# Prompt attention of a hybrid decoder layer: from one instruction stream per superblock to one stream over all superblocks

## The chip, the cores and the metric

One NeuronCore of a Trainium2 chip runs the whole kernel. The metric is the device time of one execution in microseconds (us): the median of several runs, lower is better. Where a trace is read, it is the trace of one profiled execution, whose own time is given beside it.

The engines are named as the profile names them: PE is TensorE (matrix products and transposes), PEld its weight loads, DVE is VectorE, ACT is ScalarE, POOL is GpSimd, and SP is SyncE, which only issues transfers here. SPq, POOLq and so on are the transfer queues that these engines issue to.

## The reference, cut to what matters

The reference is one inference step of one decoder layer over a prompt of 2048 tokens, with 16 learned meta tokens ahead of it, and over 8 x 8 sample tokens with a paged cache. Model width is 1024; there are 8 attention heads of 64 columns and a recurrent branch of 512 columns.

```python
def layer(x, attend, ...):
    hn = rmsnorm(x, g_mix_pre)
    q, k, v, xl, gate = jnp.split(hn @ w_in, [512, 1024, 1536, 2048], axis=-1)
    attn = attend(q, k, v)
    lru, h_last, conv_last = rglru_branch(xl, ...)
    mixed = jnp.concatenate([attn, lru * jax.nn.gelu(gate)], axis=-1) @ w_out
    x = x + rmsnorm(mixed, g_mix_post)
    u = jax.nn.relu(rmsnorm(x, g_mlp_pre) @ w_up)
    x = x + rmsnorm((u * u) @ w_down, g_mlp_post)

def sb_attend(q, q_pos, k, v, k_pos, bias):       # stick-breaking attention
    z = einsum('bqhd,bkhd->bhqk', q, k) * HEAD_DIM**-0.5 + bias
    mask = k_pos < q_pos
    log_keep = where(mask, log_sigmoid(-z), 0)
    suffix = cumsum(log_keep, axis=3, reverse=True) - log_keep
    w = where(mask, exp(log_sigmoid(z) + suffix), 0)
    return einsum('bhqk,bkhd->bqhd', w, v)
```

Attention is causal, and a weight is the product of a sigmoid with all later keep factors of its row. So keys are worked through from the last to the first, with a carry from one group of keys to the next. There is no softmax and no sum to divide by.

## The kernel before

The 2048 prompt rows are cut into four superblocks of `SB` = 512 rows (s = 0 to 3). Every float32 product is made as three products of a shorter type, high x high, high x low and low x high, so a weight tile (`wraw`) is loaded by SyncE and split into `whi` (ScalarE, L158) and `wlo` (VectorE, L159) first.

**Main stream.** It runs in this order: the input projections of superblocks 0 to 3 (`inproj`: recurrent branch and gates, keys, values, then queries); then, for each superblock, the output projection (`out_proj`), the transposes of its normed rows (`xpose`, L261), and the MLP in four slices (`up`, `down`). Its products are in `gemm` (L171 to L189; matmuls at L181, L182, L183: one tile of 512 columns takes 24 of them) and in `gemm_nat` (L191 to L224; L213, L214, L215). The keys and values of a superblock go to DRAM tiles `kd` and `vd`, its queries to `qd[s]`, and attention's output to `md[s]`, from which `load()` brings it back (`x<-md`, L955; cast to `ahi` on ScalarE at L951 and rest to `alo` at L952). The values leave their projection through `v_evac`: ScalarE copies a tile to a staging buffer `sf` (L561, stored to `out_v_prompt` by SyncE, L568) and casts it to `vst` (L564, stored to `vd`, L556).

**Side stream.** Attention is woven into the main stream. `Work` keeps a list `side` of generators, each with a key that it marks done at its end and a key that has to be ready before it starts. `work.tick(c)`, called by the products after every few matmuls, adds `c` times `work.rate` to a debt, and steps the present generator until the debt is paid; each step says how much of the debt it pays. `work.burst` steps for a given amount, and `work.need(key)` steps until `key` is done. Before the output projection of superblock s, `group(s)` calls `work.need(("a", s))`. The call for superblock 0 comes right after the first of the four query products of superblock 3. The list before is `sample_attn`, then `attn(0)` to `attn(3)`; `attn(s)` may start when `("kv", s)` is ready, which the end of superblock s's queries marks.

**One attention step.** For a head, `head()` loads its queries `q` (two buffers, L667) and its last 128 keys and values `kvt` (three buffers, L671, L672); `kv_load()` loads a group of 512 keys and values `kv` (three buffers, L684, L685, L691, L692). All of these are issued by GpSimd. Then, on each tile of 128 queries:

- logits: two matmuls into a bank `T` (L702; three banks, shared with the transposes);
- `chain`: two sigmoids on ScalarE (`keep` L640, `beta` L641), a scan on VectorE (L645, L648), the carry, and a product (L652);
- four steps later or more, `emit_T`: up to four transposes (L712) into another bank `T`, copied to `wth` by ScalarE (L723, or L719 for the group of 16 meta rows) and to `wtl` by VectorE (L724, or L720);
- four steps later or more, `emit_V`: two matmuls with the values (L734, L736) into the one bank `O`; after a head's last values ScalarE copies half of `O` (`pb`, L744), VectorE adds the other half, and SyncE stores the head to `md[s]` (L746).

A generator ends when its logits are used up and its queues of pending transposes (`tq`) and values (`vq`) are empty. So the last transposes and values of a superblock are issued before the first logits of the next.

The order on TensorE is that of the program text, with the side steps where `Work` puts them. The orders on ScalarE, VectorE, GpSimd and SyncE are made by a scheduler, which may issue a load ahead of its place in the text when its buffer is free.

Of the kernel before, what the change touches and what calls it, by code (L numbers as in the profile page):

```python
# [8 lines left out]
F32 = mybir.dt.float32  # L9
F32R = mybir.dt.float32r  # L10
# [6 lines left out]
P = 128  # L17
# [19 lines left out]
class Work:  # L37
# [7 lines left out]
    def step(self):  # L45
        while True:
# [5 lines left out]
            try:  # L52
                busy, pe = next(self.gen)
# [31 lines left out]
def _program(tc, I, O, NSB, NSC):  # L85
# [570 lines left out]
    def attn(s, K):  # L656
        live = {"w": 0, "kv": 0, "kvt": 0}
        tq, vq, heads = [], [], {}
        step = [0]

        def keys(h, a, n):
            return kd[h].rearrange("e p n -> (e p) n")[:, a:a + n]

        def head(h):
            if h < NH and h not in heads:
                q = T(att, [P, 2, SB], F32R, "q", 2)
                nc.gpsimd.dma_start(q.rearrange("p e n -> p (e n)"),  # L667
                                    qd[s][h].rearrange("p e n -> p (e n)").unsqueeze(0).to_broadcast([2, HD, 2 * SB]))
                kt = T(att, [P, 256], F32R, "kvt", 3)
                k0 = SB * s + 3 * P  # L670
                nc.gpsimd.dma_start(kt[:, 0:P], keys(h, NMETA + k0, P))  # L671
                nc.gpsimd.dma_start(kt[:, P:2 * P], vd[h, :, k0:k0 + P])  # L672
                live["kvt"] += 1
                heads[h] = {"q": q, "kt": kt, "carry": [None] * 4, "out": None}
            return heads.get(h)

        kvs = {}

        def kv_load(n):
            if n < len(groups) and n not in kvs:  # L680
                h, g = groups[n]
                t = T(att, [P, 1024], F32R, "kv", 3)
                if g == 0:
                    nc.gpsimd.dma_start(t[:, 0:400], keys(h, 0, 400))  # L684
                    nc.gpsimd.dma_start(t[:, 400:784], vd[h, :, 0:384])  # L685
                    nc.gpsimd.memset(t[:, 784:784 + P].bitcast(F32), 0.0)
                    for r in (0, 32):
                        nc.gpsimd.dma_start(t[r:r + NMETA, 784:784 + P], vmd[:, h])
                else:
                    k0 = SB * g - P  # L690
                    nc.gpsimd.dma_start(t[:, 0:512], keys(h, NMETA + k0, 512))  # L691
                    nc.gpsimd.dma_start(t[:, 512:1024], vd[h, :, k0:k0 + 512])  # L692
                kvs[n] = t
                live["kv"] += 1
# [599 lines left out]
```

## Time and profile before

| | us |
|---|---|
| runs | 2788.22, 2781.06, 2786.87 |
| median | 2786.87 |
| the profiled execution's own time | 2790.22 |
| its span | 2788.3 |
| TensorE busy | 2688.2 |
| VectorE busy | 1814.3 |
| ScalarE busy | 1451.6 |
| GpSimd busy | 515.5 |

The span is the time from the first to the last instruction of the profiled execution; its own time is 1.9 us longer. The mean granted clock of TensorE was 0.985 of full speed. The shares of busy time are means over stages with different limits: projections without attention, projections with attention, output projection, MLP with attention (until about 2147 us) and MLP alone. In the lines quoted below, `O<-wth,kv` is an instruction that writes `O` and reads `wth` and `kv`, `128*128 128x512` are the shapes of the operands, and `[2.98 <-DVE wth L720]` says that the engine had been idle for 2.98 us and that the VectorE instruction of line 720 ended this.

### The profile page before, as it was taken

The page shows a single profiled execution, that of the slowest core. Times are in us where ns is not written, and L with a number is a line of the kernel's source. Part 1 is how long each engine was busy: PE and PEld are TensorE (multiplying, and loading weights), DVE is VectorE, ACT ScalarE, POOL GpSimd, SP SyncE. Part 2 cuts the span into 40 slices and gives each one's busy share as a digit, 9 for nine tenths or more (in the row PEclk, how much of TensorE's full clock was granted, in tenths as well). Part 3 has the DMA queues.
Part 4 walks back from the last instruction along what each step waited for, and adds up shares of the span by engine and source line. Part 5 has one row for each costly group of instructions (what it writes and reads, how often), then busy time and mean ns, then how long its engine had stood idle before and what let it go on. Part 6 is the DMA issues. An engine that isn't in the chain of part 4 may idle for free.

```text
span 2788.3 us, 36998 instructions
## 1 busy us (share of the span) xinstructions
PE 2688.2 (96%) x13804; PEld 2219.4 (80%) x13804; DVE 1814.3 (65%) x2790; ACT 1451.6 (52%) x2426; POOL 515.5 (18%) x711
## 2 busy tenths in 40 slices
PE   8999988998899999999999999999999999999998
PEld 6886766777688888887788888878888887998996
DVE  5456364686777777788867777798686436433434
ACT  6556364575665655565555555665555234332332
POOL 5336361341211101112110001120000002000002
PEclk9999998999999999999999999999999999999999
DMA  4465855467534433345443333454333334322223
GB/s 161 134 208 189 261 152 171 134 169 221 166 92 128 119 115 106 106 138 154 154 110 115 103 111 103 138 162 143 105 96 104 112 119 144 99 84 77 83 84 113
DMA packets 177316, 368.23 MB, mean 132 GB/s; under 512 B 49153, under 2 KB 79361, under 8 KB 177137
## 3 DMA queue, kind: packets, MB, share of 16 engines
q1 hardware_dynamic: 103792, 287.35, 32.2%
q0 software_dynamic: 73344, 78.52, 11.3%
q8 instruction: 109, 1.79, 0.3%
q14 instruction: 71, 0.57, 0.1%
HBM read 305.51 MB, written 60.04 MB: 131 GB/s over the span
## 4 chain that ended last, share of the span: by engine, by line
PE 80%; DVE 7%; DMA 5%; POOL 3%; issue 3%; ACT 2%; SPq 0%; POOLq 0%; DVEq 0%; ACTq 0%
PE D L181 11%; PE D L183 11%; PE D L182 11%; PE D L213 10%; PE D L214 10%; PE D L215 10%; PE T L712 4%; PE T L702 4%; PE O L734 2%; PE O L736 2%; DVE wlo L159 1%; DMA md<-pb 1%; DVE pb L648 1%; POOL rstd L237 1%; DMA q<-qd 1%
## 5 line engine op out<-in xcount | busy, mean ns | idle before, releaser
L159 DVE TENSOR_TENSOR wlo<-wraw,whi 128x1024 fp32r<-128x1024 f32 x368 | 464.2, 1261 | 496.1 <-ACT whi L158 495.8
L181 PE MATMUL D<-ahi,whi 128*128 128x512 f32 (+3 forms) x1920 | 709.2, 369 | 0.0
L183 PE MATMUL D<-ahi,wlo 128*128 128x512 f32 (+3 forms) x1920 | 686.3, 357 | 2.0 <-DVE wlo L159 2.0
L182 PE MATMUL D<-alo,whi 128*128 128x512 f32 (+3 forms) x1920 | 685.0, 357 | 2.8 <-DVE alo L1017 1.5
L158 ACT CAST whi<-wraw 128x1024 fp32r<-128x1024 f32 x368 | 386.6, 1050 | 485.5 <-PE D L214 282.8
L213 PE MATMUL D<-whi,uh 128*128 128x512 f32 x1024 | 418.1, 408 | 0.0
L183 PEld LDWEIGHTS D<-ahi,wlo 128*128 128x128 f32 x1920 | 364.8, 190 | 53.2 <-DVE wlo L159 2.9
L181 PEld LDWEIGHTS D<-ahi,whi 128*128 128x128 f32 x1920 | 365.2, 190 | 51.9 <-issue 8.7
L214 PE MATMUL D<-whi,ul 128*128 128x512 f32 x1024 | 405.2, 396 | 0.0
L215 PE MATMUL D<-wlo,uh 128*128 128x512 f32 x1024 | 404.3, 395 | 0.0
L182 PEld LDWEIGHTS D<-alo,whi 128*128 128x128 f32 x1920 | 365.7, 190 | 45.5 <-DVE alo L1017 1.7
L640 ACT ACTIVATE keep<-T,nbias 128x512 f32<-128x512 f32 (+6 forms) x352 | 209.7, 596 | 241.7 <-PE T L702 234.6
L648 DVE TENSOR_TENSOR_SCAN pb<-keep,carry 128x513 f32<-128x513 f32 (+1 forms) x228 | 270.3, 1186 | 71.9 <-ACT keep L640 69.9
L724 DVE TENSOR_TENSOR wtl<-T,wth 128x512 fp32r<-128x512 f32 (+1 forms) x320 | 191.0, 603 | 73.7 <-ACT wth L723 72.6
L723 ACT CAST wth<-T 128x512 fp32r<-128x512 f32 (+1 forms) x320 | 166.1, 523 | 127.6 <-PE T L712 122.7
L215 PEld LDWEIGHTS D<-wlo,uh 128*128 128x128 f32 x1024 | 192.7, 188 | 46.7
L213 PEld LDWEIGHTS D<-whi,uh 128*128 128x128 f32 x1024 | 192.9, 188 | 39.9 <-DVE uf L1032 0.4
L214 PEld LDWEIGHTS D<-whi,ul 128*128 128x128 f32 x1024 | 193.3, 189 | 38.6
L652 DVE TENSOR_TENSOR beta<-beta,pb 128x512 f32<-128x512 f32 (+7 forms) x360 | 208.2, 578 | 0.0
L641 ACT ACTIVATE beta<-T,bias 128x512 f32<-128x512 f32 (+6 forms) x352 | 208.2, 591 | 0.0
L712 PE MATMUL T<-ident,beta 128*128 128x128 f32 (+1 forms) x1216 | 193.7, 277 | 14.1 <-ACT beta L641 7.6
L702 PE MATMUL T<-kv,q 128*128 128x512 f32 (+5 forms) x640 | 180.4, 364 | 10.3 <-ACT beta L641 4.4
(235 smaller groups left out, 3600.0 us busy)
## 6 DMA issues: line engine op xcount, KB each, us to landing
wraw<-in_w_up SPq DMA_DIRECT2D x128, 512.0 KB, 3.5
wraw<-in_w_down SPq DMA_DIRECT2D x128, 512.0 KB, 3.5
wraw<-in_w_in SPq DMA_DIRECT2D x64, 512.0 KB, 3.9
q<-qd POOLq DMA_DIRECT2D x32, 512.0 KB, 16.9
wraw<-in_w_out SPq DMA_DIRECT2D x32, 512.0 KB, 3.5
kv<-kd POOLq DMA_DIRECT2D x48, 256.0 KB, 4.1
kv<-vd POOLq DMA_DIRECT2D x48, 256.0 KB, 4.2
y<-in_x_prompt SPq DMA_DIRECT2D x16, 512.0 KB, 5.6
```

The lines of the kernel that those rows point to most:

```text
L158: nc.scalar.copy(hi, r)
L159: nc.vector.tensor_tensor(lo, r, hi.bitcast(F32), op=ALU.subtract)
L181: nc.tensor.matmul(o, whi[:, k, :], ahi(k, a, b), start=(k == 0), stop=False)
L182: nc.tensor.matmul(o, whi[:, k, :], alo(k, a, b), start=False, stop=False)
L183: nc.tensor.matmul(o, wlo[:, k, :], ahi(k, a, b), start=False, stop=(k == KC - 1))
L213: nc.tensor.matmul(o, h, whi[:, kk, :], start=st, stop=False)
L214: nc.tensor.matmul(o, l, whi[:, kk, :], start=False, stop=False)
L215: nc.tensor.matmul(o, h, wlo[:, kk, :], start=False, stop=sp)
L640: nc.scalar.activation(keep[:, o:512], S, AF.Sigmoid, bias=nbias, scale=-0.125)
L648: nc.vector.tensor_tensor_scan(pb[:, o:513][:, ::-1], kr, kr, 1.0 if carry is None else carry, op0=ALU.mult, op1=ALU.bypass)
L702: nc.tensor.matmul(o, H["q"][:, e, i * P:(i + 1) * P], kap, start=(e == 0), stop=(e == 1))
L712: nc.tensor.transpose(t[0:kn, i * P:(i + 1) * P], w[:, c0:c0 + kn], ident)
```

## The change

`attn` loses its argument s. One generator goes through all pairs of superblock and head (`order`) and all groups of keys (`groups`). The state that counts live buffers, and the tables of loaded heads and groups, are shared over all superblocks. `head(m)` and `kv_load(n)` load the m-th head and the n-th group of the whole stream, provided that `("kv", s)` is ready for its superblock; so they may load a superblock's first head and group while the one before it is still at work. The last group of superblock s is followed by the first logits of s + 1 without the queues `tq` and `vq` being emptied between. `("a", s)` is marked done when the last head's output is stored, inside `emit_V`. Where the next superblock's keys are not ready, the generator goes on with transposes and values until both queues are empty, and then tells `Work` that it has nothing to do. The last page of values of the samples' attention also calls `head(0)` and `kv_load(0)`; one call of `head(h)` that had no effect is dropped.

```diff
             try:
-                busy, pe = next(self.gen)
+                got = next(self.gen)
+                if got is None:
+                    return False
+                busy, pe = got
...
-    def attn(s, K):
-        live = {"w": 0, "kv": 0, "kvt": 0}
-        tq, vq, heads = [], [], {}
+    live = {"w": 0, "kv": 0, "kvt": 0}
+    heads, kvs = {}, {}
+    order = [(s, h) for s in range(NSB) for h in range(NH)]
+    groups = [(s, h, g) for s, h in order for g in range(s, -1, -1)]
...
+    def head(m):
+        if m < len(order) and m not in heads and ("kv", order[m][0]) in work.ready:
+            s, h = order[m]
             q = T(att, [P, 2, SB], F32R, "q", 2)
...
+    def kv_load(n):
+        if n < len(groups) and n not in kvs and ("kv", groups[n][0]) in work.ready:
+            s, h, g = groups[n]
...
+    def attn(K):
+        tq, vq = [], []
         step = [0]
-        groups = [(h, g) for h in range(NH) for g in range(s, -1, -1)]
...
                 nc.sync.dma_start(md[s][64 * (h % 2):64 * (h % 2) + 64, h // 2, :], of)
+                if h == NH - 1:
+                    work.done.add(("a", s))
...
-            for n, (h, g) in enumerate(groups):
-                H = head(h)
+            for n, (s, h, g) in enumerate(groups):
+                while ("kv", s) not in work.ready:
+                    yield "later"
+                m = order.index((s, h))
+                H = head(m)
                 if g == s:
-                    head(h + 1) if live["kvt"] < 3 else None
+                    head(m + 1) if live["kvt"] < 3 else None
...
-                head(h)
...
                     c = next(src)
-                    if c is not None:
+                    if c == "later":
+                        if not tq and not vq:
+                            yield None
+                            continue
+                    elif c is not None:
...
                     vp = page(cv, b, pp)
+                    if t_ == 3 and bb == 1 and pp == 1:
+                        head(0)
+                        kv_load(0)
...
-    for s in range(NSB):
-        work.side.append((("a", s), ("kv", s), lambda s=s: attn(s, K)))
+    work.side.append(("a", ("kv", 0), lambda: attn(K)))
```

The numbers of instructions on each engine are the same in both kernels. The orders are the same up to the last logits of superblock 0; they differ on TensorE from its row 2697 on, and on the other engines from about there. Lines of the changed kernel are numbered 3 higher than before in the products and sigmoids, 5 higher in the attention's matmuls and 16 higher at the `ahi` casts: L707 are its logits, L717 its transposes, L739 and L741 its values, L184 to L186 its `gemm`, L643 and L644 its sigmoids, L967 its `ahi` casts.

The first place is TensorE's order at the first seam. `D_6039` is the first query product of superblock 3, the last main product before the output projection of superblock 0 is opened; `kv_5485` and `kvt_5704` belong to the last head of superblock 0, and `wth_6012` is its group of 16 meta rows, the last values of that superblock. Before:

```order
L182 MATMUL D_6039<-alo_102,whi_5936 128x512
L183 MATMUL D_6039<-ahi_101,wlo_5937 128x512
L734 MATMUL O_5996<-wth_6001,kvt_5704 128x128
L736 MATMUL O_5996<-wtl_6002,kvt_5704 128x128
L734 MATMUL O_5996<-wth_6012,kv_5485 128x512
L181 MATMUL D_6039<-ahi_101,whi_5936 128x512
L182 MATMUL D_6039<-alo_102,whi_5936 128x512
```

In the changed kernel the same query product is `D_6064`, the last values are those with `wth_6127`, and `T_6111` holds logits of superblock 1:

```order
L186 MATMUL D_6064<-ahi_101,wlo_5962 128x512
L739 MATMUL O_6100<-wth_5957,kv_5485 128x512
L741 MATMUL O_6100<-wtl_5958,kv_5485 128x512
L717 MATMUL T_6103<-ident_72,beta_5753 128x128
L739 MATMUL O_6100<-wth_6008,kv_5485 128x384
L741 MATMUL O_6100<-wtl_6009,kv_5485 128x384
L707 MATMUL T_6111<-kv_5747,q_5917 128x512 x2
L717 MATMUL T_6122<-ident_72,beta_5785 16x128
L717 MATMUL T_6122<-ident_72,beta_5816 16x128
L717 MATMUL T_6122<-ident_72,beta_5840 16x128
L717 MATMUL T_6122<-ident_72,beta_5874 16x128
L739 MATMUL O_6100<-wth_6052,kv_5485 128x256
```

All of the last head's values now stand behind the last row of the query product, with logits of superblock 1 (`kv_5747`) among them, and the run goes on without a main product up to the values with `wth_6127` and four transposes of superblock 1.

The second place is ScalarE's order at the same seam. `D_5718` to `D_5721` are the four tiles of superblock 3's values, which `v_evac` copies to `sf` and casts to `vst`. Before:

```order
L561 COPY sf_5989<-D_5720 128x512
L719 CAST wth_6012<-T_6007 16x512
L158 CAST whi_6033<-wraw_5940 128x1024
L564 CAST vst_5991<-D_5720 128x8x64
L561 COPY sf_6022<-D_5721 128x512
L564 CAST vst_6024<-D_5721 128x8x64
L744 COPY pb_6052<-O_5996 64x512
```

In the changed kernel, with `keep` and `beta` the sigmoids of superblock 1:

```order
L564 COPY sf_6018<-D_5720 128x512
L161 CAST whi_6058<-wraw_5965 128x1024
L643 ACTIVATE keep_293_1888<-T_6038,nbias_188 128x384
L567 CAST vst_6020<-D_5720 128x8x64
L644 ACTIVATE beta_6041<-T_6038,bias_186 128x384
L564 COPY sf_6031<-D_5721 128x512
L728 CAST wth_6052<-T_6049 128x256
L643 ACTIVATE keep_294_1890<-T_6074,nbias_188 128x512
L567 CAST vst_6033<-D_5721 128x8x64
L644 ACTIVATE beta_6077<-T_6074,bias_186 128x512
L161 CAST whi_6181<-wraw_6062 128x1024
L728 CAST wth_6105<-T_6103 128x128
```

Sigmoids of superblock 1 and weight casts of superblock 0 now stand between and behind the evictions of superblock 3's values; the cast of the 16 rows has moved further down, behind `sh`, the eviction of the query product.

The third place is ScalarE's order where the output projection's operand is brought back (`ahi<-x`, four casts of which the second to the last are shown). Before:

```order
L951 CAST ahi_1186_6135<-x_6139 128x1024
L640 ACTIVATE keep_293_1888<-T_6247,nbias_188 128x400
L641 ACTIVATE beta_6250<-T_6247,bias_186 128x400
L158 CAST whi_6289<-wraw_6212 128x1024
L640 ACTIVATE keep_294_1890<-T_6264,nbias_188 128x400
L641 ACTIVATE beta_6267<-T_6264,bias_186 128x400
L601 CAST sh_6275<-D_6214 128x512
L951 CAST ahi_1186_6135<-x_6202 128x1024
L640 ACTIVATE keep_293_1888<-T_6307,nbias_188 128x400
L951 CAST ahi_1186_6135<-x_6206 128x1024
```

In the changed kernel:

```order
L967 CAST ahi_1191_6143<-x_6179 128x1024
L967 CAST ahi_1191_6143<-x_6220 128x1024
L643 ACTIVATE keep_293_1888<-T_6251,nbias_188 128x400
L644 ACTIVATE beta_6254<-T_6251,bias_186 128x400
L728 CAST wth_6266<-T_6262 128x384
L161 CAST whi_6290<-wraw_6230 128x1024
L604 CAST sh_6276<-D_6232 128x512
L643 ACTIVATE keep_294_1890<-T_6302,nbias_188 128x400
L644 ACTIVATE beta_6305<-T_6302,bias_186 128x400
L967 CAST ahi_1191_6143<-x_6224 128x1024
```

The third cast has moved up to stand directly behind the second, ahead of attention's sigmoids and of `sh`; the last one has moved down.

More of the change, by code (lines that the diff above doesn't have):

```diff
@@ L653, in chain @@
         return beta, cn
-    def attn(s, K):
-        live = {"w": 0, "kv": 0, "kvt": 0}
-        tq, vq, heads = [], [], {}
-        step = [0]
[L661 to L694, printed above, removed]
-        groups = [(h, g) for h in range(NH) for g in range(s, -1, -1)]
@@ new lines, in _program, with keys @@
+    live = {"w": 0, "kv": 0, "kvt": 0}
+    heads, kvs = {}, {}
+    order = [(s, h) for s in range(NSB) for h in range(NH)]
+    groups = [(s, h, g) for s, h in order for g in range(s, -1, -1)]
+    def keys(h, a, n):
+        return kd[h].rearrange("e p n -> (e p) n")[:, a:a + n]
+    def head(m):
+        if m < len(order) and m not in heads and ("kv", order[m][0]) in work.ready:
+            s, h = order[m]
+            q = T(att, [P, 2, SB], F32R, "q", 2)
+            nc.gpsimd.dma_start(q.rearrange("p e n -> p (e n)"),
+                                qd[s][h].rearrange("p e n -> p (e n)").unsqueeze(0).to_broadcast([2, HD, 2 * SB]))
+            kt = T(att, [P, 256], F32R, "kvt", 3)
+            k0 = SB * s + 3 * P
+            nc.gpsimd.dma_start(kt[:, 0:P], keys(h, NMETA + k0, P))
+            nc.gpsimd.dma_start(kt[:, P:2 * P], vd[h, :, k0:k0 + P])
+            live["kvt"] += 1
+            heads[m] = {"q": q, "kt": kt, "carry": [None] * 4, "out": None, "s": s, "h": h}
+        return heads.get(m)
@@ new lines, in kv_load @@
+    def kv_load(n):
+        if n < len(groups) and n not in kvs and ("kv", groups[n][0]) in work.ready:
+            s, h, g = groups[n]
+            t = T(att, [P, 1024], F32R, "kv", 3)
+            if g == 0:
+                nc.gpsimd.dma_start(t[:, 0:400], keys(h, 0, 400))
+                nc.gpsimd.dma_start(t[:, 400:784], vd[h, :, 0:384])
+                nc.gpsimd.memset(t[:, 784:784 + P].bitcast(F32), 0.0)
+                for r in (0, 32):
+                    nc.gpsimd.dma_start(t[r:r + NMETA, 784:784 + P], vmd[:, h])
+            else:
+                k0 = SB * g - P
+                nc.gpsimd.dma_start(t[:, 0:512], keys(h, NMETA + k0, 512))
+                nc.gpsimd.dma_start(t[:, 512:1024], vd[h, :, k0:k0 + 512])
+            kvs[n] = t
+            live["kv"] += 1
@@ L741, in emit_V @@
             if it["last"]:
-                out, h = H["out"], it["h"]
+                out, s, h = H["out"], H["s"], H["h"]
                 of = T(att, [P, 513], F32, "pb", 2)[0:64, 0:SB]
```

## The prediction

> **What bounds the kernel now.** I read the profile's page first, then busy time by stage, the seams between two superblocks' attention, and what stops TensorE there. The page gives the span and the busy time of each engine:
> ```profile
> span 2788.3 us, 36998 instructions
> PE 2688.2 (96%) x13804; PEld 2219.4 (80%) x13804; DVE 1814.3 (65%) x2790; ACT 1451.6 (52%) x2426; POOL 515.5 (18%) x711
> ```
> TensorE is the bound. The order lists of both kernels hold the same 12826 rows on TensorE and equal counts elsewhere, so the change can move the time only through TensorE's 2788.3 − 2688.2 = 100.1 us without work and through its clock. The next view divides the span into stages; the columns are length, busy PE, PEld, DVE, ACT, POOL, granted clock, DMA share, GB/s:
> ```profile
> 0.00:385.00 385.00, 364.00 (x2296) 287.21 (x2297) 205.32 (x317) 218.28 (x347) 183.17 (x209) 1.00 0.60 187
> 385.00:520.00 135.00, 109.86 (x534) 84.31 (x533) 74.62 (x126) 67.01 (x120) 38.03 (x52) 0.87 0.59 164
> 520.00:640.00 120.00, 113.57 (x530) 90.42 (x528) 91.41 (x145) 83.68 (x138) 48.62 (x60) 0.99 0.52 146
> 640.00:700.00 60.00, 52.67 (x242) 42.59 (x242) 38.70 (x63) 32.78 (x57) 8.84 (x17) 0.94 0.78 241
> 745.00:785.00 40.00, 26.46 (x117) 20.14 (x116) 33.27 (x60) 24.02 (x44) 9.83 (x16) 0.70 0.50 142
> 955.00:980.00 25.00, 25.00 (x129) 20.74 (x128) 15.70 (x26) 12.86 (x23) 4.16 (x8) 1.00 0.47 132
> 1285.00:1352.00 67.00, 60.68 (x293) 49.05 (x292) 59.79 (x90) 39.57 (x70) 20.65 (x28) 0.95 0.62 196
> 1464.00:1486.00 22.00, 22.00 (x109) 18.07 (x109) 13.72 (x22) 10.75 (x19) 3.47 (x6) 1.00 0.50 132
> 1865.00:1880.00 15.00, 12.66 (x66) 10.30 (x65) 14.59 (x24) 10.46 (x21) 8.73 (x9) 1.00 0.34 105
> 2147.00:2788.00 641.00, 623.93 (x3350) 541.71 (x3348) 274.89 (x376) 207.18 (x319) 36.16 (x36) 0.99 0.32 104
> ```
> Up to 640 us TensorE lacks 21.0 + 25.1 + 6.4 = 52.6 us. The orders agree up to the last logits of superblock 0 (TensorE's row 2697, about 633 us), so none of that moves. After 2147 us no attention is left; those 17.1 us stay. In reach are 7.3 (640 to 700), 13.5 (745 to 785), 6.3 (1285 to 1352) and 2.3 us (1865 to 1880), some 30 us, and what is lost to the clock: at most 60 × 0.06 = 3.6, 40 × 0.30 = 12 and 67 × 0.05 = 3.4 us, 19 us. So about 49 us are at stake.
>
> **The seams.** The first logits of superblocks 1, 2 and 3 (start, duration, line; a pair of matmuls each):
> ```profile
> 657.82 0.33 PE L702 MATMUL T<-kvt,q 128*128 128x128 f32 x2
> 978.85 0.33 PE L702 MATMUL T<-kvt,q 128*128 128x128 f32 x2
> 1484.59 0.34 PE L702 MATMUL T<-kvt,q 128*128 128x128 f32 x2
> ```
> The second and third seam lie in the rows 955 to 980 and 1464 to 1486: TensorE works 25.00 of 25.00 and 22.00 of 22.00 us at clock 1.00, since projection products fill it. A drained attention pipeline costs nothing there and a continuous one earns nothing. Only the first seam has idle time. TensorE there, first the first and the last of six products in a row (in brackets the idle time before an instruction and its releaser):
> ```profile
> 649.13 0.40 PE L181 MATMUL D<-ahi,whi 128*128 128x512 f32 x1
> ...
> 650.30 0.39 PE L183 MATMUL D<-ahi,wlo 128*128 128x512 f32 x1
> ...
> 653.84 0.79 PE L734 MATMUL O<-wth,kv 128*128 128x512 f32 x1 [2.98 <-DVE wth L720]
> ...
> 675.08 0.50 PE L213 MATMUL D<-whi,ahi 128*128 128x512 f32 x1 [1.67 <-ACT ahi L951]
> 676.34 0.51 PE L214 MATMUL D<-whi,alo 128*128 128x512 f32 x1 [0.77 <-DVE alo L952]
> 683.28 0.50 PE L213 MATMUL D<-whi,ahi 128*128 128x512 f32 x1 [1.92 <-DVE sl L602]
> ```
> Products start every (650.30 − 649.13) / 5 = 0.234 us. The stalls sum to 2.98 + 1.67 + 0.77 + 1.92 = 7.3 us. The granted clock after the first of them (same columns as above):
> ```profile
> 650.86:653.84 2.98, 0.00 (x1) 0.00 (x1) 0.68 (x1) 1.82 (x3) 0.57 (x1) 1.00 0.54 151
> 653.84:657.30 3.46, 3.46 (x8) 2.81 (x9) 1.92 (x2) 1.35 (x3) 1.60 (x3) 0.51 0.51 140
> ```
> A stall of 2.98 us is followed by 3.46 us at clock 0.51, where 1.7 us of work at full clock is lost. The stage's mean clock of 0.94 stands for two such stretches, so the seam now costs 7.3 + 2 × 1.7 = 10.7 us.
>
> By the Trainium skill, "TensorE: Matmul & The Clock Gate", section "Part 1: The HAM clock gate", the clock halves after an idle window of about 3.4 us and recovers after as long a busy one. The recovery agrees with the 3.46 us here; the drop after only 2.98 us does not agree with a full idle window, so the measurement decides.
>
> **What the change moves.** The tail of superblock 0 waits on ScalarE, where V's evictions sit in the same queue:
> ```profile
> 652.02 0.59 ACT L561 COPY sf<-D 128x512 f32<-128x512 f32 x1 [5.54 <-DMA out_v_prompt<-sf]
> 652.50 0.57 ACT L719 CAST wth<-T 16x512 fp32r<-16x512 f32 x1
> 655.22 0.59 ACT L564 CAST vst<-D 128x512 fp32r<-128x512 f32 x1 [1.20 <-DMA vd<-vst]
> 656.10 0.59 ACT L561 COPY sf<-D 128x512 f32<-128x512 f32 x1 [0.28 <-DMA out_v_prompt<-sf]
> 657.70 0.59 ACT L564 CAST vst<-D 128x512 fp32r<-128x512 f32 x1 [1.02 <-DMA vd<-vst]
> 660.15 1.06 ACT L158 CAST whi<-wraw 128x1024 fp32r<-128x1024 f32 x1
> 662.03 0.62 ACT L601 CAST sh<-D 128x512 fp32r<-128x512 f32 x1
> 673.98 1.04 ACT L951 CAST ahi<-x 128x1024 fp32r<-128x1024 f32 x1 [5.92 <-DMA x<-md]
> 685.58 1.04 ACT L951 CAST ahi<-x 128x1024 fp32r<-128x1024 f32 x1 [3.12 <-DMA x<-md]
> ```
> The copy at 652.02 waits 5.54 us for a store to free its staging buffer, and the 16-row weight cast behind it makes TensorE's 2.98-us stall.
>
> Loads first. The change can issue `q`, `kvt` and `kv` of the next superblock earlier, but they are issued ahead already:
> ```profile
> 613.34 0.80 POOL L667 DMA_DIRECT2D q<-qd  x1 [0.26 <-PE T L702]
> 958.69 0.82 POOL L667 DMA_DIRECT2D q<-qd  x1 [7.29 <-PE T L702]
> ```
> The first is superblock 1's, 44 us before its first logits; the second is a head of superblock 2, 20 us before that superblock's. GpSimd's order through the seams is all but unchanged, and nothing waits there for these loads. I cost this part, and the two calls in the samples' attention, at zero. What covers them is the scheduler's hoisting; without it a seam would pay one load's flight.
>
> Now TensorE's order. Superblock 1's logits are drawn among superblock 0's last transposes and values, so these come later in the instruction stream: before, the last value product stood among the first query product's 24 matmuls; now it stands behind all of them, in a run of 20 rows that `need(("a",0))` empties before out_proj's group is opened, with no projection product among them.
>
> Step by step, with ScalarE's evictions ending when they do now, since stores free their buffers. Products fill TensorE until about 653.9 us: the present stall began at 650.86, 15 products of 0.234 us (3.5) are now ahead of it, some 1.2 us of value products are put off, and 0.7 us of logits come in. Then the run:
> - A transpose needs the bank that a `beta` behind the eviction at 655.22 frees: ready at 656.4. Two value products end at 654.4, so 2.0 to 2.4 us of idle time.
> - The next logits wait for a weight cast behind the copy at 656.10 (0.8), the 16-row transposes for a `beta` behind the eviction at 657.70 (0.7), and the diagonal values for a cast behind the weight split at 660.15 (0.9).
> - The last value product needs the 16-row cast, which now stands behind `sh` (0.62) and one more pair of sigmoids: 2.4 us. The four transposes behind it share that wait.
>
> Sum 2.4 + 0.8 + 0.7 + 0.9 + 2.4 = 7.2 us, where the old order had 2.98. The clock: the longest stalls are just under 2.98 us, but they lie close together; between no half-clock stretch and two (3.4 us) I take 2.5. By the Trainium skill's rule named above it would be nothing, and out_proj's 1.7 below too, and the seam would come out level with today.
>
> Then out_proj's start. Superblock 0's last `md` store goes out about 4 us later, but the first `x<-md` load does not need the last heads, so I take the 1.67 + 0.77 us as gone. On ScalarE the third `ahi` cast now stands directly behind the second with sigmoids and `sh` queued behind it; its `x` buffer waits for a load, today up to 3.12 us. That makes 1.9 to 5 us, I take 3.5, and one half-clock stretch of 1.7.
>
> After: 7.2 + 2.5 + 3.5 + 1.7 = 14.9 us against 10.7 now: **+4 us**. Bounds: at best every stall but the bank waits overlaps (about 4 us in all: −7); at worst each store wait comes once more (+10).
>
> Further places. Attention runs about 18 to 24 product rows (4 to 6 us) ahead of before against the main stream from here on. The stalls it meets later:
> ```profile
> 754.29 1.03 PE L702 MATMUL T<-kv,q 128*128 128x400 f32 x2 [4.43 <-ACT beta L641]
> 762.15 0.48 PE L261 MATMUL T<-ident,y 128*128 128x128 f32 x1 [4.57 <-DVE y L1003]
> 1302.13 0.47 PE L712 MATMUL T<-ident,beta 128*128 128x128 f32 x2 [3.06 <-DVE wtl L724]
> 1326.86 1.11 PE L261 MATMUL T<-ident,y 128*128 128x128 f32 x4 [2.60 <-ACT beta L641]
> ```
> At 745 to 785 TensorE waits for out_proj's rows `y`; that chain runs from out_proj's end and is not touched. One more logits pair of 400 columns stands ahead of the first transposes. −4 to +5, I take +0.5. At 1285 to 1352 and 1865 to 1880 the order's patterns are the same, shifted; a shift can hit or miss these stalls, ±6 us around 0.
>
> The sum is about +4 us. The profiled execution took 2790.2 us (span 2788.3 and 1.9 around it), 3.4 above the median of 2786.9; the shift applied to the median gives **2791 us**.
>
> **The rivals.**
> - *Continuous attention fills the seams* (faster, 0.20). If the in-line logits let the last casts overlap with products, seam 1's 10.7 us go: 2776. If the shift also spares one of the stalls at 1285 to 1352 with its clock, another 6: 2770. For it: idle time of 49 us in reach. Against it: two of three seams are saturated, and the run behind the first query product has no products to cover it. The Trainium skill, "Trainium Kernel Development and Optimization", section "Best Practices", asks for double buffering so that transfers lie beside compute, which speaks for the change; the three load rows above show that already done here.
> - *The run waits on V's stores* (slower, 0.18). The price: one more wait of the length of that 5.54 us, in the run of TensorE without cover, with its 1.7 us of half clock, on top of +4: 2798; with the third `ahi` cast held for its 3.12 us as well, 2801. It decides if a store frees its staging buffer later than today by more than the 4 us that separate the forecast from the 0.3% bound.
> - *Nothing happens* (0.17): loads issued already, two seams full, the first seam's waits only change places: 2787.
>
> **How the numbers follow.** My forecast (a few us at seam 1) has 0.45, of which 0.07 beyond 0.3%. About 0.3% (8.4 us) is what a measurement of this kernel can tell from no change, as its runs spread from 2781 to 2788. Faster: 0.20. Within 0.3%: 0.38 + 0.17 = 0.55. Slower: 0.07 + 0.18 = 0.25. The likeliest case alone gives 2780 (the −7) to 2797 (the +10). The range takes in the slower rival and two us of the shift beside it, 2803, and reaches at the low end past the 10.7 us, 2775; left out are the far half of the faster rival (0.10) and mishaps above 2803 (0.05).
>
> **What would show it.** In the new trace: the span unchanged up to about 633 us; windows of the second and third seam full; in seam 1 the last value product of superblock 0 near 663 us instead of 653.8, with several stalls of 0.7 to 2.4 us ahead of it, put down to `beta`, `wth` or `wtl`; out_proj's first product without the 1.67-us wait, a wait for `ahi` or `sl` some us later. I am wrong if seam 1's idle time falls below 5 us, if it rises above 20, or if the total moves by over 8 us at 745 to 785 or 1285 to 1352, where I have taken the shift as neutral.

## The result, and the profile after

The changed kernel takes 2793.32 us (median of 22 runs, 2788.61 to 2801.09), the kernel before 2786.89 us (22 runs, 2781.06 to 2794.96). The ratio is 1.0022, with a 95% interval of 1.0015 to 1.0028: 6.4 us slower. The interval leaves out 1, so the change is clear of the noise, though it stays within the 0.3% that the prediction counted as no change. The profiled execution of the changed kernel has a span of 2792.3 us. Its page, span and busy time:

```profile
span 2792.3 us, 37004 instructions
PE 2685.4 (96%) x13804; PEld 2216.5 (79%) x13804; DVE 1818.9 (65%) x2790; ACT 1449.8 (52%) x2426; POOL 515.1 (18%) x711
```

Up to the last logits of superblock 0 the two kernels have the same orders, and there the changed kernel's profiled execution happens to be 1.9 us ahead: those logits start at 633.11 us before and 631.17 after. At the end it is 4.0 us behind (2792.3 against 2788.3). So the part that the change touches costs about 5.9 us in these two executions, close to the 6.4 us of the medians. The stages of the changed kernel (length, busy PE, PEld, DVE, ACT, POOL, granted clock, DMA share, GB/s):

```profile
640.00:700.00 60.00, 52.67 (x237) 42.54 (x236) 38.78 (x66) 31.28 (x56) 8.84 (x19) 0.89 0.82 245
745.00:785.00 40.00, 25.64 (x116) 19.45 (x115) 33.51 (x60) 24.50 (x45) 10.54 (x16) 0.70 0.44 137
955.00:980.00 25.00, 25.00 (x131) 20.90 (x130) 17.33 (x31) 12.27 (x23) 3.48 (x6) 1.00 0.48 128
1285.00:1352.00 67.00, 60.24 (x294) 48.55 (x293) 61.12 (x96) 39.17 (x72) 21.78 (x29) 0.95 0.64 203
1464.00:1486.00 22.00, 22.00 (x110) 18.18 (x109) 16.30 (x29) 12.56 (x24) 1.60 (x3) 1.00 0.41 119
1865.00:1880.00 15.00, 12.39 (x68) 9.80 (x68) 14.52 (x25) 9.53 (x19) 7.63 (x8) 1.00 0.16 45
1880.00:2147.00 267.00, 263.82 (x1267) 216.90 (x1266) 198.88 (x299) 147.50 (x244) 19.77 (x38) 1.00 0.36 109
```

The last of these rows has a counterpart of before that was not shown yet:

```profile
1880.00:2147.00 267.00, 267.00 (x1288) 220.36 (x1287) 202.41 (x308) 150.54 (x249) 19.75 (x38) 1.00 0.36 109
```

TensorE's idle time at the first seam is 7.33 us in both kernels. The windows at the second and third seam are full in both. At 745 to 785 it grows by 0.8, at 1285 to 1352 by 0.4, at 1865 to 1880 by 0.3 us. At 1880 to 2147, where it was nothing before, it is 3.2 us. That stage has the largest difference, and it holds no seam. With the +1.1 us of the first seam, which is worked out below, these differences make 5.8 of the 5.9 us.

The first seam in the changed kernel, TensorE's stalls (start, duration, line; idle time before it and releaser), and the clock behind them:

```profile
654.59 0.33 PE L717 MATMUL T<-ident,beta 128*128 128x128 f32 x1 [2.28 <-ACT beta L644]
656.02 1.22 PE L707 MATMUL T<-kv,q 128*128 128x512 f32 x2 [0.74 <-DVE wtl L729]
660.26 0.47 PE L741 MATMUL O<-wtl,kvt 128*128 128x128 f32 x1 [1.63 <-DVE wtl L729]
663.40 0.79 PE L739 MATMUL O<-wth,kv 128*128 128x512 f32 x1 [2.67 <-DVE wth L725]
```

```profile
655.60:669.30 13.70, 8.98 (x26) 6.87 (x27) 10.69 (x20) 6.60 (x13) 2.27 (x5) 0.50 0.96 300
669.30:690.00 20.70, 20.70 (x98) 17.07 (x97) 15.63 (x22) 12.65 (x19) 0.81 (x1) 1.00 0.78 239
```

The run of value products waits four times, 2.28 + 0.74 + 1.63 + 2.67 = 7.3 us, and 8.98 us of work run at clock 0.50, which loses 4.5 us. Then TensorE is full through the start of the output projection, where it stood three times before. So the seam costs 7.3 + 4.5 = 11.8 us, against 10.7 before: +1.1 us.

The last two waits, 4.3 of the 7.3 us, end on VectorE. ScalarE's cast of the 16 rows, then, on VectorE, the two instructions that TensorE waits for; each takes the rest that a cast leaves:

```profile
659.51 0.56 ACT L724 CAST wth<-T 16x512 fp32r<-16x512 f32 x1
```
```profile
659.92 0.28 DVE L729 TENSOR_TENSOR wtl<-T,wth 128x128 fp32r<-128x128 f32 x1
662.67 0.68 DVE L725 TENSOR_TENSOR wth<-T,wth 16x512 fp32r<-16x512 f32 x1
```

The cast is done at 660.07 us, its rest starts 2.6 us later. VectorE works without a gap from 654.70 to 663.35 us there: superblock 1's scans and products, a weight split (1.22 us, ahead of the first of the two rests) and the rest of the query product (ahead of the second).

All these are differences of two single traces. Among the runs described below that do not edit this place, TensorE's idle time from 640 to 700 us is 5.6 to 8.6 us at a mean clock of 0.91 to 0.97 in six traces with the old order at the first seam, and 7.2 to 7.8 us at 0.89 to 0.91 in four with the new one. In the mean that is 0.1 us more of idle time and 60 × 0.04 = 2.4 us of clock, so the seam costs some 1 to 3 us. The +0.8, +0.4 and +0.3 us are less than traces of one order differ by. The stall in the last stage is clear of that: with the load of queries that is named below, TensorE has no idle time from 1880 to 1935 us in three traces with the old order at all seams (the kernel before, `drain_all`, `nov_before`), and 2.6 to 5.7 us in four with the new order at some or all (the changed kernel, `nov_after`, `drain_23`, `drain_1`).

The new stall lies near 1897 us. First TensorE and VectorE there, then SyncE's issues and one of GpSimd's, all of the changed kernel:

```profile
1899.42 0.63 PE L707 MATMUL T<-kv,q 128*128 128x384 f32 x2 [2.67 <-DVE wtl L729]
```
```profile
1896.03 1.28 DVE L1106 SCALAR_TENSOR_TENSOR x<-acc,rstd,x 128x1024 f32<-128x1024 f32 x1 [7.46 <-DMA x<-x1d]
```
```profile
1880.51 2.14 SPq L1107 DMA_DIRECT2D out_y_prompt<-x  x2
1883.45 0.34 SPq L152 DMA_DIRECT2D wraw<-in_w_up  x1
1888.02 3.20 SPq L257 DMA_DIRECT2D x<-x1d  x2
```
```profile
1876.49 0.86 POOL L672 DMA_DIRECT2D q<-qd  x1 [0.31 <-PE T L717]
```

And the same issues in the kernel before, SyncE and GpSimd:

```profile
1877.72 2.09 SPq L1091 DMA_DIRECT2D out_y_prompt<-x  x2
1880.40 2.37 SPq L254 DMA_DIRECT2D x<-x1d  x2
```
```profile
1883.58 0.87 POOL L667 DMA_DIRECT2D q<-qd  x1 [8.99 <-issue]
```

This is the end of superblock 1's MLP. Two `x` buffers hold the reloaded residual rows; VectorE adds, SyncE stores y from the same buffer, and the buffer takes the next reload (`x<-x1d`) when that store has landed. In the kernel before the reloads go out 2.7 us after the stores (1877.72 to 1880.40). In the changed kernel it takes 7.5 us (1880.51 to 1888.02), and the first reload arrives 8 us later, where the two of the kernel before took 4.7 and 4.8 us. The next addition holds VectorE for 7.46 us, with attention's `wtl` behind it in VectorE's queue, and TensorE runs dry 2.67 us before that `wtl` comes. What has moved against these stores is the load of a later head's queries: it goes out 4 us ahead of them in the changed kernel and 6 us behind them in the kernel before. These loads are under way for long. In the kernel before (count, size, median us from issue to landing over the whole execution):

```profile
q<-qd POOLq DMA_DIRECT2D x32, 512.0 KB, 17.3
x<-x1d SPq DMA_DIRECT2D x12, 512.0 KB, 4.7
out_y_prompt<-x SPq DMA_DIRECT2D x12, 512.0 KB, 3.0
```

### The profile page after: what moved, and what is told of

Same layout as the page of the kernel before. It is cut to its first block, busy times and chain, and to the rows that moved or that the text cites. A ratio compares the mean times of both kernels' runs of the same rounds, so it can differ in the third digit from the quotient of the medians.

```text
span 2792.3 us, 37004 instructions
## 1 busy us (share of the span) xinstructions
PE 2685.4 (96%) x13804; PEld 2216.5 (79%) x13804; DVE 1818.9 (65%) x2790; ACT 1449.8 (52%) x2426; POOL 515.1 (18%) x711
## 4 chain that ended last, share of the span: by engine, by line
PE 78%; DVE 8%; DMA 5%; POOL 3%; issue 3%; ACT 3%; SPq 0%; another core or an unknown queue 0%; POOLq 0%; DVEq 0%; ACTq 0%
PE D L184 11%; PE D L186 11%; PE D L185 11%; PE D L216 10%; PE D L217 10%; PE D L218 10%; PE T L717 4%; PE T L707 4%; PE O L739 2%; PE O L741 2%; DVE wlo L162 1%; DVE pb L651 1%; DMA vd<-vst 1%; POOL rstd L240 1%; DVE beta L655 1%
## 5 line engine op out<-in xcount | busy, mean ns | idle before, releaser
L184 PE MATMUL D<-ahi,whi 128*128 128x512 f32 (+3 forms) x1920 | 709.1, 369 | 0.0
L186 PE MATMUL D<-ahi,wlo 128*128 128x512 f32 (+3 forms) x1920 | 686.0, 357 | 2.5 <-DVE wlo L162 2.5
L186 PEld LDWEIGHTS D<-ahi,wlo 128*128 128x128 f32 x1920 | 364.1, 190 | 53.6 <-DVE wlo L162 3.4
L184 PEld LDWEIGHTS D<-ahi,whi 128*128 128x128 f32 x1920 | 364.8, 190 | 51.4 <-issue 8.7
L643 ACT ACTIVATE keep<-T,nbias 128x512 f32<-128x512 f32 (+6 forms) x352 | 210.0, 597 | 226.7 <-PE T L707 221.7
L644 ACT ACTIVATE beta<-T,bias 128x512 f32<-128x512 f32 (+6 forms) x352 | 208.4, 592 | 0.0
L717 PE MATMUL T<-ident,beta 128*128 128x128 f32 (+1 forms) x1216 | 194.4, 278 | 14.1 <-ACT beta L644 9.6
L707 PE MATMUL T<-kv,q 128*128 128x512 f32 (+5 forms) x640 | 180.8, 365 | 12.3 <-DVE wtl L729 6.6
## 6 DMA issues: line engine op xcount, KB each, us to landing
q<-qd POOLq DMA_DIRECT2D x32, 512.0 KB, 17.3
```

The lines of the kernel that those rows point to most:

```text
L184: nc.tensor.matmul(o, whi[:, k, :], ahi(k, a, b), start=(k == 0), stop=False)
L186: nc.tensor.matmul(o, wlo[:, k, :], ahi(k, a, b), start=False, stop=(k == KC - 1))
L707: nc.tensor.matmul(o, H["q"][:, e, i * P:(i + 1) * P], kap, start=(e == 0), stop=(e == 1))
L717: nc.tensor.transpose(t[0:kn, i * P:(i + 1) * P], w[:, c0:c0 + kn], ident)
```

## The experiments

Three theories were tried against each other. *The seam*: the run of value products without cover makes the loss. *The collision*: attention now runs some us ahead of the main stream, and one of its loads meets the store and the reload at 1880 us. *Many small stalls*: no place stands out. Each run is compared with runs of the kernel before on the same chip.

**Emptying the queues at all seams** (`drain_all`), and at some of them (`drain_23`, `drain_1`). The edit of the first; the other two have (2, 3) and (1,) as the superblocks ahead of whose first logits the queues are emptied:

```diff
                 while ("kv", s) not in work.ready:
                     yield "later"
+                if h == 0 and g == s and s in (1, 2, 3):
+                    while tq or vq:
+                        yield None
+                    yield None
```

> The changed kernel, but the generator empties its queues of transposes and values at all three seams before the next superblock's first logits. All instruction orders are then those of the kernel before, on every engine; what is left of the change is the shared state and the way it is told that keys are ready. Theory (the seams' order makes the whole difference): ratio to the kernel before 1.000, within 0.1%, so about 6 us faster than the changed kernel. Rival (something else in the change costs time): 1.002.

Measured: 2785.24 us, ratio 1.0001 (0.9989 to 1.0012). The shared state, the loads called in the samples' attention and the way readiness is told cost nothing that an interval of ±0.1% (3 us) would show; the order at the seams makes the difference.

> The changed kernel with the queues emptied at the second and third seam only, so in line at the first seam. Theory A (the first seam itself costs little, about +1 us of clock, and the rest of the +6 us is a shift of attention against the main stream that meets later stalls differently, above all at 1880 to 1930 us): +1 to +3 us, and no wait of VectorE for an x load of several us near 1890. Rival B (the run of 20 rows without products at the first seam makes nearly all of it): +5 to +7 us, and TensorE's idle time between 640 and 700 us some 5 us above the 7.3 us of before.

> The changed kernel with the queues emptied at the first seam only, so in line at the second and third seam. Both seams are full of products, so no idle time there in either theory. Theory A (later stalls meet the shifted attention differently): 0 to +5 us, all of it behind 1000 us, at 1285 to 1352 or at 1860 to 1930. Rival B (the first seam makes nearly all): within 1 us of the kernel before.

Measured: in line at the first seam alone 2789.69 us, ratio 1.0014 (1.0005 to 1.0023), some +4 us. In line at the second and third seam alone 2797.76 us, ratio 1.0049 (1.0034 to 1.0065), some +14 us. Rival B falls: the first seam is not needed for the loss, and its idle time did not rise. Both seams that are full of products before and after bring the larger loss, and the two losses do not add up, since all three seams in line give +6 us. `drain_23` missed one part of theory A's expectation: it has a stall near 1890 too, of 2.92 us. There the load of queries goes out between the stores (1874.00 us) and the reload (1877.55), at 1876.55, and the reload lands after 10.0 us; this run was not repeated without that load. `drain_1` went far beyond theory A's 0 to +5 us, but at a place that the theory named. Its stall is the largest; TensorE and VectorE:

```profile
1895.81 1.12 PE L717 MATMUL T<-ident,beta 128*128 128x128 f32 x4 [5.75 <-DVE wtl L729]
```
```profile
1893.87 1.28 DVE L1110 SCALAR_TENSOR_TENSOR x<-acc,rstd,x 128x1024 f32<-128x1024 f32 x1 [9.83 <-DMA x<-x1d]
```

SyncE's issues of the same run, and GpSimd's load of the queries:

```profile
1879.33 1.53 SPq L1111 DMA_DIRECT2D out_y_prompt<-x  x2
1886.83 0.33 SPq L257 DMA_DIRECT2D x<-x1d  x1
```
```profile
1875.52 0.87 POOL L672 DMA_DIRECT2D q<-qd  x1 [0.53 <-PE T L717]
```

Store to reload again takes 7.5 us, with the queries' load 4 us ahead of the stores. No weight load stands between the two on SyncE here, so that the one in the changed kernel is not what delays the reload.

**V's stores** (`nov_before`, `nov_after`). The edit:

```diff
-            if t < 4:
+            if t < 4 and s < NSB - 1:
                 nc.sync.dma_start(O["v_prompt"][pos0 + P * t:pos0 + P * t + P, :], vf)
```

> The kernel before without the stores of superblock 3's rows of v_prompt (that part of the output is left out), so that the staging copies on ScalarE wait for no store at the first seam. If V's stores make the first seam's stall: the 2.98 us before the last values of superblock 0 and the half-clock stretch behind it (1.7 us) go, -4 to -5 us. If another wait stands right behind (the stores to vd, the weight cast): 0 to -2 us.

> The changed kernel without the same stores. If V's stores make the waits in the run without products: of 2.3 + 0.7 + 1.6 + 2.7 us the first two go, and the time comes to within 3 us of the kernel before. If the run is made by its own chain (weight cast, sh, sigmoids, scan): the idle time of 640 to 700 us stays at 6 to 7 us and the time at +5 to +6 us.

Measured: 2785.58 us, ratio 0.9999 (0.9989 to 1.0010), and 2793.45 us, ratio 1.0022 (1.0010 to 1.0033). The time moves in neither kernel. ScalarE in the two, the cast that feeds the other store of the values:

```profile
650.18 0.59 ACT L564 CAST vst<-D 128x512 fp32r<-128x512 f32 x1 [7.34 <-DMA vd<-vst]
```
```profile
648.83 0.59 ACT L567 CAST vst<-D 128x512 fp32r<-128x512 f32 x1 [7.31 <-DMA vd<-vst]
```

The staging copy no longer waits, and the cast behind it waits for its own store instead. In `nov_before` it starts 21.9 us behind the last logits of superblock 0 (628.32 us); with the stores it started 22.1 us behind them (655.22 after 633.11). The 2.98 us before the last values are gone in `nov_before`, but TensorE still waits 5.7 us from 640 to 700 us, up to 2.2 us at a time, for `beta`, `whi` and `wlo`; in `nov_after` it waits 7.8 us. So leaving out one store of the two gains nothing; what happens without both was not tried.

**Cover for the run** (`gate_before`, `gate_after`). The output projection of superblock 0 is opened one query product later:

```diff
+    next(queries)
     cur = group(0)
     ld = cur.load()
-    for c in range(1, NQ):
+    for c in range(2, NQ):
...
-NQ = 3
+NQ = 4
```

> The kernel before with the output projection of superblock 0 opened one query product later (after the second), and all four query products ahead of it, so that two products still cover the loads. In the old order the last values of superblock 0 stand within the first product anyway: within 3 us of the kernel before, unless the moved weight loads cost something.

> The changed kernel with the same edit: the last values of superblock 0 now have the second query product among them. If the missing cover makes the first seam's idle time (7.3 us) and its 13.7 us at half clock: idle time from 640 to 700 us falls below 4 us, the half-clock stretch to one of 3.4 us, and the time to within 2 us of the same edit made to the kernel before. If not: the two stay 5 to 7 us apart.

Measured: 2800.0 us, ratio 1.0045 (1.0030 to 1.0061), and 2799.13 us, ratio 1.0044 (1.0027 to 1.0061). The edit costs both kernels, which I had not expected. Windows of the first seam and of the output projection's end, the kernel before with the edit and the changed one with it:

```profile
640.00:700.00 60.00, 50.06 (x217) 40.02 (x216) 37.63 (x59) 30.40 (x53) 6.12 (x12) 0.89 0.82 248
745.00:785.00 40.00, 21.26 (x92) 16.32 (x90) 31.54 (x58) 22.77 (x46) 8.93 (x12) 0.66 0.42 130
```
```profile
640.00:700.00 60.00, 51.45 (x226) 40.81 (x226) 36.31 (x61) 29.18 (x52) 7.38 (x14) 0.91 0.85 253
745.00:785.00 40.00, 20.82 (x100) 15.38 (x99) 32.98 (x62) 23.50 (x45) 12.18 (x18) 0.70 0.43 135
```

The idle time of the first seam does not fall below 4 us as it should have with cover (8.6 us in the changed kernel, 9.9 in the other), and 19 us instead of 13.5 are lost at 745 to 785, where the transposes of the rows `y` wait. The two kernels come out level, but as the edit added a loss of twice the size to be explained, this says little about the run itself: it does not show that the missing cover is what the seam costs.

**The collision itself** (`noq_before`, `noq_after`, `noq_drain_1`). The load in question has 512 KB and is that of head 6 of superblock 3. The orders on TensorE, ScalarE, VectorE and SyncE stay as they are:

```diff
+            if (s, h) == (3, 6):
+                nc.gpsimd.memset(q.rearrange("p e n -> p (e n)").bitcast(F32), 0.0)
+            else:
-            nc.gpsimd.dma_start(q.rearrange("p e n -> p (e n)"), ...)
+                nc.gpsimd.dma_start(q.rearrange("p e n -> p (e n)"), ...)
```

> The kernel before with one transfer left out: the queries of head 6 of superblock 3 are not loaded but set to zero (that head's result is of zero queries). All orders stay. In the kernel before that load goes out at 1883.6 us, behind the reloads of x1d. Theory (the load collides with superblock 1's y stores and x1d reloads only in the changed kernel): within 1 us of the kernel before. Rival: no other expectation here; this is the control.

> The changed kernel with the same transfer left out. There it goes out at 1876.5 us, 4 us ahead of the y stores. Theory: store and reload become quick again (store to reload 3 us instead of 7.5), VectorE's wait of 7.5 us for x1d falls to 2 us or less, TensorE's stall of 2.67 us goes, -2 to -4 us, so +2 to +4 us against the kernel before. Rival (the weight load between stores and reloads on SyncE, or the order on VectorE, makes the wait): the wait stays at 5 us or more and the time within 1 us of the changed kernel.

> The kernel that is in line at the second and third seam only, with the queries of head 6 of superblock 3 set to zero instead of loaded. Before this edit it ran 13 us longer than the kernel before in its own call (ratio 1.0049), with VectorE waiting 9.8 us for x1d and TensorE standing 5.75 us at 1890 us and at half clock for 6.8 us behind it. Theory (that load's collision with the reload): wait and stall go, -6 to -10 us, to within 3 to 7 us of the kernel before. Rival (the reload is late for another reason): the stall stays above 4 us.

Measured: `noq_before` 2789.72 us, ratio 1.0006 (0.9992 to 1.0020); `noq_after` 2787.95 us, ratio 1.0008 (0.9995 to 1.0020); `noq_drain_1` 2791.91 us, ratio 1.0016 (1.0004 to 1.0027). SyncE and VectorE in `noq_after`, then VectorE in `noq_drain_1`:

```profile
1876.60 2.14 SPq L1110 DMA_DIRECT2D out_y_prompt<-x  x2
1879.53 0.34 SPq L152 DMA_DIRECT2D wraw<-in_w_up  x1
1879.96 2.53 SPq L257 DMA_DIRECT2D x<-x1d  x2
```
```profile
1885.66 1.28 DVE L1109 SCALAR_TENSOR_TENSOR x<-acc,rstd,x 128x1024 f32<-128x1024 f32 x1 [1.00 <-DMA x<-x1d]
```
```profile
1889.40 1.28 DVE L1113 SCALAR_TENSOR_TENSOR x<-acc,rstd,x 128x1024 f32<-128x1024 f32 x1 [2.43 <-DMA x<-x1d]
```

The window from 1880 to 1935 us in the changed kernel, in `noq_after`, in `drain_1` and in `noq_drain_1`:

```profile
1880.00:1935.00 55.00, 51.82 (x250) 42.18 (x249) 42.97 (x65) 29.62 (x52) 4.13 (x7) 1.00 0.51 164
```
```profile
1880.00:1935.00 55.00, 55.00 (x268) 45.50 (x267) 45.91 (x70) 34.14 (x58) 4.98 (x10) 1.00 0.50 157
```
```profile
1880.00:1935.00 55.00, 49.26 (x232) 40.58 (x231) 39.88 (x63) 29.23 (x51) 2.72 (x5) 0.94 0.44 144
```
```profile
1880.00:1935.00 55.00, 55.00 (x272) 45.65 (x271) 44.02 (x70) 32.85 (x56) 5.52 (x9) 1.00 0.42 136
```

Without that one load the reload follows the stores after 3.4 us, with the same weight load between them on SyncE as in the changed kernel. VectorE's wait falls from 7.46 to 1.00 us, and from 9.83 to 2.43 in the kernel that is in line at the later seams only; TensorE's stall is gone in both. `drain_1` loses 5.75 us of idle time and 55 × 0.06 = 3.3 us of clock there, 9.1 us, and its ratio falls by 0.0033, 9.2 us. The changed kernel gains 0.0014, 3.9 us, for 3.2 us of idle time in the trace. The second difference has an interval of ±0.0014 and is only just clear of nothing; the first, with ±0.0019, is well clear. Of the 14 us of `drain_1` some 4.5 stay, and where they lie was not looked into. The control `noq_before` was expected within 1 us; it came to 1.7, with an interval from −2 to +6.

The other traces with this load agree. Where it goes out 3.8 to 6.6 us ahead of the stores (the changed kernel, `nov_after`, `gate_after`, `drain_1`, `pool_after`), store to reload takes 7.0 to 7.5 us. Where it goes out 5.9 to 8.2 us behind them (the kernel before, `nov_before`, `gate_before`, `drain_all`, `pool_before`), it takes 2.6 to 3.4 us. That this load delays the reload, and the reload TensorE, is shown; which resource the transfers share is not.

Leaving out the load also leaves the changed kernel's ratio and that of `noq_before` level, 1.0008 and 1.0006; with intervals of ±0.0013 that is consistent with a rest of 1 to 3 us, which the runs cannot tell from nothing.

**The addition off VectorE** (`pool_before`, `pool_after`):

```diff
-                    nc.vector.scalar_tensor_tensor(xt, acc, r, xt, op0=ALU.mult, op1=ALU.add)
+                    nc.scalar.activation(acc, acc, AF.Identity, scale=r)
+                    nc.gpsimd.tensor_tensor(xt, acc, xt, op=ALU.add)
```

> The kernel before with the residual additions at the end of an MLP taken off VectorE: ScalarE scales by rstd, GpSimd adds the reloaded x1d. TensorE's order stays. Theory (VectorE does not wait there in the kernel before): 0 to -2 us, from 12 instructions of 1.28 us less on VectorE.

> The changed kernel with the same edit, so that no instruction of attention on VectorE stands behind a wait for x1d, whatever makes the reload late. Theory (the reload's delay reaches TensorE through VectorE's queue): the stall near 1897 us goes and the time falls by 3 to 5 us, to within 3 us of the same edit made to the kernel before. Rival (the remaining difference is spread over many small stalls): it stays 5 to 7 us above that.

Measured: 2794.77 us, ratio 1.0019 (1.0007 to 1.0032), and 2795.32 us, ratio 1.0034 (1.0022 to 1.0046). In the changed kernel the stall near 1897 us goes, as expected (idle time from 1880 to 1935 us falls from 3.2 to 1.1 us). But the edit costs the kernel before 5 us, where I had expected a gain. The changed one takes 3 us more than without it, which its interval (0.0012 ± 0.0014) does not tell from nothing. The edit gives the kernel before a stall of its own in the same place:

```profile
1892.65 0.50 PE L736 MATMUL O<-wtl,kv 128*128 128x512 f32 x1 [2.41 <-DVE wtl L724]
```

What holds that `wtl` is a scan of attention, ahead of it on VectorE, that runs beside the two additions now on GpSimd:

```profile
1885.63 5.70 DVE L648 TENSOR_TENSOR_SCAN pb<-keep,carry 128x401 f32<-128x401 f32 x1
1885.71 4.76 POOL L1091 TENSOR_TENSOR x<-acc,x 128x1024 f32<-128x1024 f32 x2
```

With no such addition beside it, a scan of the same shape takes 1.05 us at 1881.06 in the same trace. So the additions seem to slow VectorE from GpSimd as well; that is read from this trace and was not tested.

The two edited kernels differ by 0.0015 ± 0.0017, 4 us, so the expected narrowing to within 3 us is not shown. This is no better version. A way that keeps VectorE's work and ends the chain of store and reload (writing the sum over `acc` and storing y from there, so that `x` is free once read) was not tried.

## Why the prediction was right or wrong

The total was forecast at +4 us, 2791, and is +6.4, 2793.3. That the sum came this close is luck: the first seam was put at +4 us and came to +1.1 (1 to 3 by all traces), and the shift of attention, put at nothing, made a stall of 3.2 us elsewhere.

- *Loads ahead of the seam and the calls in the samples' attention, at zero*: right. With all seams emptied the ratio is 1.0001. (The prediction speaks of three load rows; it shows two.)
- *Second and third seam full, nothing to win or lose there*: right for the windows, wrong as an argument for the rest. Being in line there brings attention ahead, and by itself (`drain_1`) that costs the 14 us of which 9 lie at 1880 to 1935.
- *The run of value products, 7.2 us of waits*: right in sum, 7.3, and nearly in each part (2.4, 0.8, 0.7, 0.9, 2.4 against 2.28, 0.74, none, 1.63, 2.67). The reason named for the first holds: a bank freed by a `beta` behind V's evictions. For the last two the prediction looked at ScalarE's queue, and it is VectorE's that ends them: the 16-row cast behind `sh` was done 2.6 us before VectorE came to its rest. That the lengths agree is luck in part. And the store of `v_prompt`, from which the eviction's time was taken, can be left out without a change in time.
- *Clock, 2.5 us and 1.7 more*: 4.5 measured against 4.2 in all, though it lies wholly in and behind the run. Why it is so much is said below.
- *Out_proj's start, 3.5 us of waits for the third `ahi` cast*: wrong. The stalls of 1.67, 0.77 and 1.92 us all go and none takes their place. The queue on ScalarE does stand behind that cast, but the cast waits 1.32 us for its load and not 1.9 to 5, and TensorE has query products to do in the meantime and is full from 669 to 690 us. So the seam came to +1.1 us, not +4.
- *745 to 785, +0.5*: +0.8 of idle time at the same clock. *1285 to 1352 and 1865 to 1880, 0*: +0.4 and +0.3.
- *The shift of attention, taken as neutral, ±6 us*: here the prediction was wrong in kind. The stages were weighed by the stalls that they already had; the shift made one in a stretch that was full before, at 1880 to 1935, by bringing a load of queries ahead of a store. That is +3.2 us, the largest single term. The bounds held it, the place was not foreseen.

The slower rival named the right sort of mechanism, a store that holds a buffer longer, in the wrong place: at the first seam leaving out the stores of `v_prompt` changes nothing, and at the end of an MLP y's store decides. The faster rival had its 10.7 us of the first seam; the change trades them for 11.8.

On the clock: the Trainium skill, "TensorE: Matmul & The Clock Gate", section "Part 1: The HAM clock gate", calls the window of activity free-running. The traces agree with that part: in each of the 14, all half-clock stretches up to the last matmul start and end on a grid of 3.41 us, which lies differently in each execution. I counted the time without a matmul in each window of that grid, from 60 us on. At full clock, all 146 windows with 1.9 us or more of it are followed by half clock, and none of the 10572 with less than 1.4 us; between these limits 12 of 80 are. At half clock, all 147 windows with 0.8 us or more are followed by another one. So the full idle window that the prediction quotes is not needed here, and the place of a stall on the grid decides.

The stall of 2.67 us from 1896.75 in the changed kernel lies across two windows, 1.35 us in one and 1.32 in the next, and the clock stays full:

```profile
1894.69:1898.10 3.41, 2.06 (x9) 1.34 (x8) 2.07 (x2) 0.00 (x0) 0.00 (x0) 1.00 0.21 76
1898.10:1901.51 3.41, 2.09 (x10) 1.80 (x11) 3.41 (x8) 1.25 (x3) 0.00 (x0) 1.00 0.93 312
```

Of the stall of 2.60 us from 1892.36 in `nov_after`, in the same place of the program, 2.35 us lie in one window, and the next one is at half clock:

```profile
1891.30:1894.72 3.42, 1.06 (x5) 0.55 (x3) 3.15 (x4) 0.00 (x0) 0.00 (x0) 1.00 0.39 151
1894.72:1898.13 3.41, 3.16 (x8) 2.68 (x9) 3.41 (x7) 2.33 (x5) 0.00 (x0) 0.50 0.83 228
```

A single stall of such a length thus costs nothing, or one window at half clock (at most 1.7 us), or two: of the 2.92 us in `drain_23`, 1.98 lie in one window and 0.94 in the next, and 6.8 us at half clock follow. Only a mean belongs in a sum. Stalls close together keep the clock down: in the run of value products three half-clock windows in a row hold 0.81, 2.94 and 0.93 us without a matmul, so that four windows, 13.7 us, pass before the clock returns.

## What to carry to other kernels

Joining two software pipelines at their seam can pay only where the bounding engine is idle at the seam, and need not even there: here the 7.3 us of idle time only changed places. Look at that window first, and at the queues of all engines that the joined work passes. When work is woven into a busy stream, a change of its order shifts all that follows against that stream: go through the chains of store and reload through few buffers, and see which large loads of the shifted work will now fall ahead of them. A stall that such a shift makes can be tested by itself, by leaving out the one transfer with every order kept.

## What the runs showed of the hardware

One load of 512 KB, itself of a kind that takes 17.3 us to land (median), lengthened the way from a store of 512 KB to the reload of its buffer to 7.5 us when it was issued 4 us ahead; issued 6 us behind the store it left that way at 2.7 us, and without it the way took 3.4 us. Leaving out one of two stores that feed on the same evictions (1 MB less to write) moved no time: the other store's wait of 7.3 us took its place. Half clock came in whole windows of a grid of 3.41 us, after every window with 1.9 us or more without a matmul and after none with less than 1.4 us. And a scan on VectorE beside two additions on GpSimd took 5.70 us instead of 1.05.
